# Output projection of a hybrid decoder layer: seven products of sums of quarters in place of eight products of quarters

## The chip, the cores and the metric

The kernel runs on one core of one Trainium2 chip. The metric is device time in microseconds (us). Five engines work side by side, each through its own list of instructions in order: TensorE (PE, matrix products), VectorE (DVE), ScalarE (ACT), GpSimd (POOL, here almost only an issuer of loads) and SyncE (SP, the issuer of most loads). They wait for each other through semaphores.

## What is computed

The layer normalises x (256 tokens, 2048 features), multiplies by one wide input matrix, runs two token mixers beside each other (a gated delta rule and block attention), widens both, merges them through two sigmoid gates and projects the result once more. All of it is float32. The change concerns the last lines:

```python
u_a = oa @ w_branch_a
...
u_b = ob @ w_branch_b
merged = jax.nn.sigmoid(gate_a) * u_a + jax.nn.sigmoid(gate_b) * u_b
return merged @ w_out          # 256 x 2048 times 2048 x 2048
...
x = x + rms_norm(y, post_norm_w[l])
```

## The kernel before

**Split products.** TensorE multiplies in a reduced float32 form (float32r). To keep float32 accuracy each operand is split in a high and a low part: `split` (L218 to L223) lets ScalarE copy the high part (L221) and VectorE subtract it from the whole for the low part (L222). A product of two split operands is three matrix products: high by high, high by low, low by high. The weights pass through three buffers for the high and three for the low parts (pool `wspl`), the raw weights through three buffers of 1 MB (pool `wraw`), loaded by SP.

**The projections with tokens on the partitions** go through `proj_n` (L360 to L377): 512 output columns, two banks of PSUM (one for each tile of 128 tokens). For every four k-tiles (of 128 rows of the weights) one load of 1 MB, in two halves; each half is split once (128 x 1024) and feeds 12 matrix products of 128 x 128 by 128 x 512: two k-tiles, two token tiles, three products each. After every k-tile `tick()` runs the queues of side work, which are Python generators that say after how many k-tiles their next piece comes (a unit is two k-tiles).

**The last stages** are four rounds of two projections, here called ua0, ub0, ... ua3, ub3 (L897 to L905; 8 k-tiles each, 48 products), and the output projection y0 to y3 (L937 to L969; 16 k-tiles, 96 products each). After each ua VectorE multiplies the gate `ga` by its two banks (L900), after each ub it multiplies `gb` by its banks (L903) and adds (L904); that is a quarter of the columns of the merged matrix. `merge(c)` (L884 to L895) then turns this quarter with TensorE (four transposes for each token tile, "mt", L141) and splits it into `mT`, ScalarE the high part (L893) and VectorE the low one (L894). It runs in pieces during the next projection: the second quarter's during ua2, the last one's during y0. So k-tiles 4c to 4c + 3 of the output projection come from `merge(c)`.

The output projection takes its weights through `proj_n` for the column blocks 0 to 2, and `weigh` (L915) squares and weighs the two banks of a block after it (ScalarE L918, VectorE L922, with `postw`, loaded by POOL long before). The last block keeps its split weights and goes through one token tile after the other (L943 to L969), and `finish` adds the residual `hx` (POOL's load) and stores.

**What sets the order.** Products and transposes keep the order in which they are written (`pin`), and so do some operations of the other engines. The rest of VectorE's, ScalarE's and the loads' instructions are put in order by a scheduler when the kernel is built; on the chip each engine follows that order strictly. In its order for the kernel before, both low parts for the first k-tiles of ub2 stand ahead of the multiplications by ua2's banks.

## Time and profile before

| what | value |
| --- | --- |
| runs | 786.99 us median of 3 (786.76 to 787.74) |
| span of the profiled execution, first to last instruction | 786.4 us (its whole time is not recorded; the runs' median lies 0.6 us above this span) |
| busy: TensorE, VectorE, ScalarE | 774.7, 509.6, 403.0 us |
| first product of the output projection starts | 690.19 us |
| loads in all | 143.85 MB read, 187 GB/s over the span |

The profile's page gives busy times, the chain of work that ended last, and groups of instructions; other views of the same trace list instructions in order of time. A row of such a timeline is: start in us, duration in us, engine, line, operation, output<-inputs, shape, and in brackets how long the engine was idle before it and what it had waited for. "PEld" is TensorE's loading of the stationary operand. In a chain the columns are start, duration and work; in a table of windows they are the window, its length, then busy time and count of PE, PEld, DVE, ACT and POOL, the granted clock, the share of DMA and GB/s. Durations overlap a little for instructions in a row on one engine, so the distance from start to start is what one costs.

### The profile page before, as it was taken

How to read it: one execution, taken by the hardware profiler on the slowest of the kernel's cores; microseconds unless marked ns; L12 is line 12 of the kernel's file. 1: busy time of each engine (PE TensorE's matmuls, PEld its weight loads, DVE VectorE, ACT ScalarE, POOL GpSimd, SP SyncE). 2: the span in 40 equal slices, each digit the busy share in tenths (PEclk: the TensorE clock that was granted, in tenths of full speed). 3: DMA queues.
4: the chain of work that ended last, by engine and by line, in shares of the span. 5: the costliest groups of instructions: out<-in, count | busy, mean ns of one | idle time of the engine just before them, and what ended most of it. 6: DMA issues, size and time to landing. Idle time of an engine off the chain costs nothing.

```text
span 786.4 us, 10111 instructions
## 1 busy us (share of the span) xinstructions
PE 774.7 (99%) x3881; PEld 651.8 (83%) x3881; DVE 509.6 (65%) x849; ACT 403.0 (51%) x610; POOL 23.6 (3%) x50
## 2 busy tenths in 40 slices
PE   8999999999999999999999999999999999999995
PEld 6878888888888888888888988888888888888884
DVE  4877886785868898864446565555644666665563
ACT  4777665554745444455355647454454444444451
POOL 3010000100110000020000000000000000000000
PEclk9999999999999999999999999999999999999998
DMA  8756655665596656676435465555455554575542
GB/s 261 252 168 214 186 188 165 198 188 161 174 266 220 210 166 208 199 228 197 117 117 169 153 215 161 182 165 189 161 190 175 175 206 164 196 285 205 172 158 107
DMA packets 94960, 147.67 MB, mean 188 GB/s; under 512 B 5120, under 2 KB 47152, under 8 KB 94272
## 3 DMA queue, kind: packets, MB, share of 16 engines
q1 hardware_dynamic: 92528, 137.50, 54.3%
q0 software_dynamic: 1808, 8.48, 3.9%
q10 hardware_dynamic: 576, 1.05, 0.4%
q8 instruction: 30, 0.49, 0.3%
q14 instruction: 18, 0.15, 0.1%
HBM read 143.85 MB, written 3.17 MB: 187 GB/s over the span
## 4 chain that ended last, share of the span: by engine, by line
PE 96%; DMA 2%; ACT 1%; DVE 0%; SPq 0%; issue 0%; DVEq 0%; ACTq 0%
PE a_ga L138 11%; PE a_gb L138 11%; PE a_y L138 11%; PE a_mk L138 6%; PE a_v L138 6%; PE a_mq L138 6%; PE a_ua L138 6%; PE a_zg L138 6%; PE a_zm L138 6%; PE a_ub L138 6%; PE a_q L138 5%; PE a_k L138 5%; PE a_mv L138 5%; DMA x<-in_x_dram 2%; PE sv L138 2%; PE s L138 1%
## 5 line engine op out<-in xcount | busy, mean ns | idle before, releaser
L138 PE MATMUL a_ga<-hi_ga,hT 128*128 128x512 f32 x256 | 82.2, 394 | 0.0
L138 PE MATMUL a_gb<-hi_gb,hT 128*128 128x512 f32 x256 | 82.1, 394 | 0.0
L222 DVE TENSOR_TENSOR lo_gb<-raw_gb,hi_gb 128x1024 fp32r<-128x1024 f32 x32 | 39.2, 1224 | 41.1 <-ACT hi_gb L221 41.1
L138 PE MATMUL a_y<-hi_y,mT 128*128 128x512 f32 x208 | 65.1, 390 | 0.0
L221 ACT CAST hi_gb<-raw_gb 128x1024 fp32r<-128x1024 f32 x32 | 33.7, 1052 | 48.5 <-PE a_gb L138 34.5
L222 DVE TENSOR_TENSOR lo_ga<-raw_ga,hi_ga 128x1024 fp32r<-128x1024 f32 x32 | 39.0, 1223 | 29.4 <-ACT hi_ga L221 29.4
L221 ACT CAST hi_ga<-raw_ga 128x1024 fp32r<-128x1024 f32 x32 | 33.5, 1051 | 46.3 <-PE a_ga L138 30.3
L138 PEld LDWEIGHTS a_ga<-hi_ga,hT 128*128 128x128 f32 x256 | 48.0, 188 | 11.0 <-issue 1.0
L138 PEld LDWEIGHTS a_gb<-hi_gb,hT 128*128 128x128 f32 x256 | 48.1, 188 | 10.0
L222 DVE TENSOR_TENSOR lo_y<-raw_y,hi_y 128x1024 fp32r<-128x1024 f32 x26 | 31.7, 1224 | 29.6 <-ACT hi_y L221 29.6
L138 PE MATMUL a_ga<-lo_ga,hT 128*128 128x512 f32 x128 | 50.0, 391 | 0.0
L138 PE MATMUL a_gb<-lo_gb,hT 128*128 128x512 f32 x128 | 49.8, 389 | 0.0
L138 PE MATMUL a_k<-hT,hi_k 128*128 128x512 f32 x128 | 46.8, 406 | 0.1
L138 PE MATMUL a_q<-hT,hi_q 128*128 128x512 f32 x128 | 46.6, 404 | 0.0
L138 PE MATMUL a_mk<-hT,hi_mk 128*128 128x512 f32 x128 | 46.1, 401 | 0.0
L138 PEld LDWEIGHTS a_y<-hi_y,mT 128*128 128x128 f32 x208 | 39.0, 188 | 8.1
L138 PE MATMUL a_mq<-hT,hi_mq 128*128 128x512 f32 x128 | 45.7, 400 | 0.0
L138 PE MATMUL a_v<-hT,hi_v 128*128 128x512 f32 x128 | 45.3, 397 | 0.0
L221 ACT CAST hi_y<-raw_y 128x1024 fp32r<-128x1024 f32 x26 | 27.3, 1054 | 34.6 <-PE a_y L138 29.6
L138 PE MATMUL a_ua<-hi_ua,oaT 128*128 128x512 f32 x128 | 41.8, 395 | 0.0
L138 PE MATMUL a_zg<-hi_zg,hT 128*128 128x512 f32 x128 | 40.6, 391 | 0.0
L138 PE MATMUL a_zm<-hi_zm,hT 128*128 128x512 f32 x128 | 40.5, 392 | 0.0
(286 smaller groups left out, 1873.8 us busy)
## 6 DMA issues: line engine op xcount, KB each, us to landing
raw_ga<-in_w_in_dram SPq DMA_DIRECT2D x16, 1024.0 KB, 5.2
raw_gb<-in_w_in_dram SPq DMA_DIRECT2D x16, 1024.0 KB, 5.1
raw_y<-in_w_out_dram SPq DMA_DIRECT2D x16, 1024.0 KB, 5.0
raw_mv<-in_w_in_dram SPq DMA_DIRECT2D x8, 1024.0 KB, 5.5
raw_zg<-in_w_in_dram SPq DMA_DIRECT2D x8, 1024.0 KB, 5.1
raw_v<-in_w_in_dram SPq DMA_DIRECT2D x8, 1024.0 KB, 5.6
raw_zm<-in_w_in_dram SPq DMA_DIRECT2D x8, 1024.0 KB, 5.0
raw_mq<-in_w_in_dram SPq DMA_DIRECT2D x8, 1024.0 KB, 5.7
```

Of the source, the lines that this page charges most:

```text
L138: return pin(nc.tensor.matmul(*args, **kwargs))
L221: nc.scalar.copy(hi, raw)
L222: nc.vector.tensor_tensor(lo, raw, hi.bitcast(F32), op=ALU.subtract)
```

## The change

Of the output projection, the part that belongs to column blocks 0 and 1 and to k-tiles 0 to 7 is a product of 2 x 2 quarters: the token tiles 0 and 1, times the k-tile groups h = 0 and 1, times the column blocks c = 0 and 1. Before, its eight quarter products are part of y0 and y1 (four k-tiles, 12 matrix products each). Now seven products of sums and differences of quarters are made (Winograd's form of Strassen's scheme), and their results are added into the four result banks. The k-tiles 8 to 15 of both blocks, block 2 and block 3 are computed as before.

- `merge(0)` also copies its two token tiles into `sums_f`; `merge(1)` forms four sums of quarters of the merged matrix on VectorE, splits each (ScalarE the high parts, VectorE the low ones), and has POOL load a third quarter of the weights.
- POOL loads two other quarters of the weights earlier, and `differences()`, a queue of its own that is served by the same ticks, makes three differences of quarters on VectorE, in six operations of 128 x 1024.
- `product` does one of the seven products: two halves, each split and fed to 6 matrix products with one token tile; the same function does k-tiles 8 to 15 with both token tiles, 12 matrix products for each split half.
- The results gather in four banks; two are copied out by ScalarE on the way (`s1`, `s5`), VectorE adds into one bank and into `v`, and adds `s1` and `v` back at the end of each block. A fourth difference of weight quarters is made between the products.
- `postw` and `hx` are loaded after these products; POOL's queue holds three loads of 1 MB more, SP's one less.

```diff
     def merge(c):
         yield 1
+        p3s = []
         for t in range(NT):
...
             nc.vector.tensor_tensor(lo, p3, hi.bitcast(F32), op=ALU.subtract)
+            if c == 0:
+                nc.scalar.copy(sf[:, t], p3)
             yield 0.5
+        if c == 1:
+            nc.vector.tensor_tensor(sf[:, 2], p3s[1], sf[:, 1], op=ALU.add)
+            nc.vector.tensor_tensor(sf[:, 3], sf[:, 2], sf[:, 0], op=ALU.subtract)
+            nc.vector.tensor_tensor(sf[:, 1], sf[:, 0], sf[:, 1], op=ALU.subtract)
+            nc.vector.tensor_tensor(sf[:, 0], p3s[0], sf[:, 3], op=ALU.subtract)
+            yield 0.5
+            for i, j in enumerate((2, 3, 1, 0)):
+                nc.scalar.copy(SH[i], sf[:, j])
+                nc.vector.tensor_tensor(SL[i], sf[:, j], SH[i].bitcast(F32), op=ALU.subtract)
+                yield 0.5
+            load_quarter(0, 0, 1)
+            formed.append(True)
+            sq.add(differences())
...
+    load_quarter(1, 1, 1)
+    load_quarter(2, 0, 0)
+
+    def differences():
+        yield 4
+        for o, a, b in ((0, 0, 2), (1, 1, 0), (2, 1, 2)):
+            for u in range(2):
+                us = slice(2 * u, 2 * u + 2)
+                nc.vector.tensor_tensor(tq[o][:, us], tq[a][:, us], tq[b][:, us], op=ALU.subtract)
+                yield 2
...
+    def product(a, raw, banks, first, name):
+        for u in range(2):
+            hi, lo = split(raw[:, 2 * u : 2 * u + 2, :], [P, 2, 512], f"{name}_{u}")
+            for kk in range(2):
+                k = 2 * u + kk
+                for (ah, al), pt, new in zip(a, banks, first):
+                    mm(pt, ah[:, k], hi[:, kk, :], start=(new and k == 0), stop=False, skip_group_check=True)
+                    mm(pt, ah[:, k], lo[:, kk, :], start=False, stop=False, skip_group_check=True)
+                    mm(pt, al[:, k], hi[:, kk, :], start=False, stop=(k == 3), skip_group_check=True)
+                tick()
...
+    product([quarter(0, 0)], load(0, 0), [c21], [True], "yp1")
+    product([s_[0]], tq[0], [c12], [True], "yp5")
+    nc.scalar.copy(s1, c21)
+    raw21 = load(1, 0)
+    product([s_[1]], tq[1], [c21], [False], "yp6")
+    nc.scalar.copy(s5, c12)
+    product([quarter(0, 1)], raw21, [c11], [True], "yp2")
+    nc.vector.tensor_tensor(c12, c21, s5, op=ALU.add)
+    for u in range(2):
+        us = slice(2 * u, 2 * u + 2)
+        nc.vector.tensor_tensor(tq[1][:, us], raw21[:, us], tq[1][:, us], op=ALU.subtract)
+    product([s_[2]], tq[2], [c21], [False], "yp7")
+    product([s_[3]], load(1, 1), [c12], [False], "yp3")
+    nc.vector.tensor_tensor(v, c21, s5, op=ALU.add)
+    product([quarter(1, 1)], tq[1], [c21], [False], "yp4")
...
-    for c in range(3):
-        pts = proj_n(wo, c * 512, mT, KT, f"y{c}")
-        if c < 2:
-            for t in range(NT):
-                weigh(c, t, pts[t])
+    mq.drain()
+    for c, banks, late in ((0, (c11, c21), (c11, s1)), (1, (c12, c22), (c22, v))):
+        for h in range(2, 4):
+            product([quarter(0, h), quarter(1, h)], load(h, c), banks, [False, c == 1 and h == 2], f"y{c}_{h}")
+        nc.vector.tensor_tensor(late[0], late[0], late[1], op=ALU.add)
+        for t in range(NT):
+            weigh(c, t, banks[t])
+    pts = proj_n(wo, 2 * 512, mT, KT, "y2")
```

The products are named after the code: product 1 (yp1), 5, 6, 2, 7, 3, 4, in this order. Each call of `product` names its left factor, its weights and its bank.

More of the change, by code (lines that the diff above doesn't have):

```diff
@@ L128, in hybrid_layer @@
     after = [0]
+    extra = []
     def tick():
         after[0] -= 0.5
-        for q in (gq, vq, mq, *aq):
+        for q in (gq, vq, mq, *aq, *extra):
             q.tick()
@@ L882, in hybrid_layer, with load_quarter @@
     mT = big.tile([P, KT, 2 * S], F32R, tag="hT", name="mT")
+    sums = [big.tile([P, 2, 4, P], F32R, tag=tg, name=f"sum_{tg}") for tg in ("tt", "tv", "tw")]
+    SH = [tl[:, 0] for tl in sums] + [wk.tile([P, 4, P], F32R, tag="s", name="sum4_hi")]
+    SL = [tl[:, 1] for tl in sums] + [wk.tile([P, 4, P], F32R, tag="s", name="sum4_lo")]
+    sf = big.tile([P, 4, 4, P], F32, tag="z0", name="sums_f")
+    tq = [None, None, None]
+    def load_quarter(i, h, c):
+        tq[i] = big.tile([P, 4, 512], F32, tag=f"z{i}", name=f"tq_{i}")
+        nc.gpsimd.dma_start(
+            tq[i], wo[h * 512 : (h + 1) * 512, c * 512 : (c + 1) * 512].rearrange("(k p) c -> p k c", p=P)
+        )
+    load_quarter(1, 1, 1)
[7 more added lines that the diff above has]
+                yield 2
     def merge(c):
         yield 1
+        p3s = []
         for t in range(NT):
@@ L890, in merge @@
             p3 = pt.rearrange("p (k n) -> p k n", n=P)
+            p3s.append(p3)
             hi = mT[:, 4 * c : 4 * c + 4, t * P : (t + 1) * P]
@@ L894, in merge @@
             nc.vector.tensor_tensor(lo, p3, hi.bitcast(F32), op=ALU.subtract)
+            if c == 0:
+                nc.scalar.copy(sf[:, t], p3)
             yield 0.5
+        if c == 1:
[11 more added lines that the diff above has]
+            sq.add(differences())
+    formed = []
+    sq = Queue()
+    extra.append(sq)
     for c in range(D // 512):
@@ L905, in hybrid_layer, with quarter, load @@
         mq.add(merge(c))
+    sq.drain()
+    while not formed:
+        mq.tick()
+    def quarter(t, h):
+        ks = slice(4 * h, 4 * h + 4)
+        return mT[:, ks, t * P : (t + 1) * P], mT[:, ks, S + t * P : S + (t + 1) * P]
+    def load(h, c):
+        raw = wraw.tile([P, 4, 512], F32, tag="raw", name=f"raw_y{c}_{h}")
+        nc.sync.dma_start(raw, wo[h * 512 : (h + 1) * 512, c * 512 : (c + 1) * 512].rearrange("(k p) c -> p k c", p=P))
+        return raw
+    def product(a, raw, banks, first, name):
[8 more added lines that the diff above has]
+                tick()
+    c21, c11, c12, c22 = (acc_tile(f"a_y{n}") for n in ("21", "11", "12", "22"))
+    kept = big.tile([P, 3, 512], F32, tag="u1", name="kept")
+    s1, s5, v = (kept[:, i] for i in range(3))
+    s_ = list(zip(SH, SL))
+    product([quarter(0, 0)], load(0, 0), [c21], [True], "yp1")
[13 more added lines that the diff above has]
+    product([quarter(1, 1)], tq[1], [c21], [False], "yp4")
     postw = big.tile([P, D], F32, tag="z2", name="postw")
```

## The prediction

> **What bounds the kernel now.** I read the page first (busy shares, chain), then the chain in order of time from 600 us on, the windows of the last stages, and the timelines of VectorE (DVE), ScalarE (ACT) and TensorE (PE) around the edit.

> ```profile
> span 786.4 us, 10111 instructions
> ...
> PE 774.7 (99%) x3881; PEld 651.8 (83%) x3881; DVE 509.6 (65%) x849; ACT 403.0 (51%) x610; POOL 23.6 (3%) x50
> ...
> PE 96%; DMA 2%; ACT 1%; DVE 0%; SPq 0%; issue 0%; DVEq 0%; ACTq 0%
> ```

> ```profile
> 656.77 10.88 PE a_ub L138 x48
> ...
> 690.35 2.72 PE a_y L138 x12
> 693.07 0.44 PE mt L141 x4
> ...
> 695.34 83.00 PE a_y L138 x366
> ```

> ```profile
> 644.95:656.77 11.82, 11.82 (x57) 9.79 (x57) 8.48 (x11) 5.29 (x6) 0.00 (x0) 1.00 0.50 177
> 656.77:667.65 10.88, 10.88 (x49) 9.01 (x49) 6.09 (x7) 4.22 (x4) 0.00 (x0) 1.00 0.57 194
> 690.35:712.99 22.64, 22.64 (x105) 18.74 (x105) 13.01 (x14) 10.09 (x12) 0.72 (x1) 1.00 0.77 279
> ```

> TensorE is 96% of the chain, and from 600 us to the last product nothing else stands in it: 366 products take 83.00 us, **0.2268 us each**, also where many in a row go into one bank (the last block). So a product less is 0.227 us less, as long as TensorE never has to wait. The windows say how much room there is: VectorE is busy 8.48 of 11.82 us in the third product with the first branch (ua2), 6.09 of 10.88 in ub2, 13.01 of 22.64 in the first output block.

> **What is removed.** Eight quarter products of 12 matrix products (4 k-tiles, three each) become seven: 12 x 0.2268 = **-2.72 us**. The rest of the chain keeps its products. Everything else in the change is work for VectorE, ScalarE and the queues, and the question is whether TensorE waits for it. It does, at two places.

> **Place one: the start of ub2.** The sums of the quarters of the merged matrix hang on the second merge, which runs during ua2. In the kernel before, this stretch looks like this (VectorE, then TensorE, then ScalarE):

> ```profile
> 649.94 1.35 DVE L894 TENSOR_TENSOR mT<-mt,mT 128x512 fp32r<-128x512 f32 x2
> 652.45 1.23 DVE L222 TENSOR_TENSOR lo_ub<-raw_ub,hi_ub 128x1024 fp32r<-128x1024 f32 x1 [1.17 <-ACT hi_ub L221]
> 655.17 1.23 DVE L222 TENSOR_TENSOR lo_ub<-raw_ub,hi_ub 128x1024 fp32r<-128x1024 f32 x1 [1.50 <-ACT hi_ub L221]
> 656.32 0.68 DVE L900 TENSOR_TENSOR ga<-ga,a_ua 128x512 f32<-128x512 f32 x1
> ```

> ```profile
> 656.38 0.39 PE L138 MATMUL a_ua<-hi_ua,oaT 128*128 128x512 f32 x1
> 656.61 0.39 PE L138 MATMUL a_ub<-hi_ub,obT 128*128 128x512 f32 x1
> ...
> 656.83 0.39 PE L138 MATMUL a_ub<-lo_ub,obT 128*128 128x512 f32 x1
> ```

> ```profile
> 649.98 0.59 ACT L893 CAST mT<-mt 128x512 fp32r<-128x512 f32 x1 [0.73 <-PE mt L141]
> 651.37 1.05 ACT L221 CAST hi_ub<-raw_ub 128x1024 fp32r<-128x1024 f32 x1 [0.80 <-PE a_ua L138]
> 654.09 1.05 ACT L221 CAST hi_ub<-raw_ub 128x1024 fp32r<-128x1024 f32 x1 [1.67 <-PE a_ua L138]
> ```

> Two low parts for ub2 are ready before ua2 ends, and only then come the multiplications by ua2's result (L900), which must wait for ua2's last product. In the order that the scheduler makes of the changed kernel, eight new operations of 512 columns (four sums, four low parts of the sums) stand behind the two mT operations, then **both multiplications, and only behind these the first low part for ub2**. A low part behind an operation that waits for the end of ua2 cannot be early. For its time I need the pitch of VectorE's operations in a row:

> ```profile
> 689.90 1.28 DVE L903 TENSOR_TENSOR gb<-gb,a_ub 128x512 f32<-128x512 f32 x2
> 691.09 1.29 DVE L904 TENSOR_TENSOR ga<-ga,gb 128x512 f32<-128x512 f32 x2
> 692.30 1.22 DVE L222 TENSOR_TENSOR lo_y<-raw_y,hi_y 128x1024 fp32r<-128x1024 f32 x1
> ```

> ```profile
> 760.47 2.35 DVE L955 TENSOR_TENSOR keep_u<-raw_y,keep_u 128x1024 fp32r<-128x1024 f32 x2
> 762.73 2.35 DVE L222 TENSOR_TENSOR lo_y<-raw_y,hi_y 128x1024 fp32r<-128x1024 f32 x2
> ```

> Two operations of 512 take 1.20 us, two of 1024 take 2.26: 0.60 and **1.13 us** from start to start, 0.68 and 1.22 to the end of one. The hand-over from TensorE to ScalarE and the price of a late operand come from these:

> ```profile
> 689.96 0.39 PE L138 MATMUL a_ub<-hi_ub,obT 128*128 128x512 f32 x1
> ...
> 690.19 0.39 PE L138 MATMUL a_y<-hi_y,mT 128*128 128x512 f32 x1
> ...
> 690.39 1.06 ACT L221 CAST hi_y<-raw_y 128x1024 fp32r<-128x1024 f32 x1 [1.67 <-PE a_ub L138]
> ```

> ```profile
> 6.61 0.69 DVE L277 TENSOR_TENSOR lo_k<-rawf_k,hi_k 128x512 fp32r<-128x512 f32 x1
> ...
> 7.35 0.29 PEld L138 LDWEIGHTS a_k<-hT,lo_k 128*128 128x128 f32 x1 [0.44 <-DVE lo_k L277]
> 7.36 0.58 PE L138 MATMUL a_k<-hT,lo_k 128*128 128x256 f32 x1
> ...
> 7.73 0.63 PE L138 MATMUL a_k<-hT,hi_k 128*128 128x512 f32 x1
> ```

> ```profile
> 8.16 0.41 PE L138 MATMUL a_k<-hT,lo_k 128*128 128x256 f32 x1
> 8.37 0.63 PE L138 MATMUL a_k<-hT,hi_k 128*128 128x512 f32 x1
> ```

> A product issued at 689.96 ends at 690.35 and ScalarE starts at 690.39: 0.04 us. A low part that ended at 7.30 let TensorE go on at 7.35: 0.05 us, and the late product held TensorE 0.37 us where the same shape holds it 0.21: up to 0.16 us more, since its weights were not loaded ahead. I take 0.10 for that at the later, faster pace.

> Now the sum for ub2, on the clock of before. The second mT operation waits for its copy (650.57) and starts at 650.61; the sums follow. The last of the four low parts waits for the fourth high copy, which ScalarE does behind hi_ub (654.09 plus a pitch of 0.95): 655.04 to 655.63. So that low part starts at 655.67, the multiplications at 656.27 and 656.87 (ua2's last product ends at 656.77, so without any sums the second would start at 656.81: the order alone carries the wait), the low part for ub2 at 657.47. It ends at 658.69; plus 0.05 and 0.10, the second product of ub2 goes at 658.84 in place of 656.83: **+2.0 us**. VectorE then makes a low part per 1.13 us and TensorE takes one per 12 products, 2.72 us, so the lead is regained.

> **Place two: the seven products.** A half quarter of weights now feeds 6 products (1.36 us) instead of 12 (2.72 us), but still costs VectorE a low part of 1.13 us, and two differences, one sum and two mT operations stand between them. In the changed order, all in one row from 692.30 on (pitches as above; mT 0.65, from the pair's 1.35): lo of product 5 at 692.30, mT 693.43, lo 694.08, mT 695.21, product 6 at 695.86 and 696.99, difference 698.12, product 2 at 699.25 and 700.38, sum 701.51, difference 702.11, first lo of product 7 at **703.24**, end 704.46. ScalarE keeps up: the tightest, the high part for product 6 behind the copy of product 1's bank, is ready at 695.82. With nothing in its way TensorE would want product 7's low part at 702.19 (690.19, four quarter products of 2.72, 0.88 us of mt, one product), so it waits 2.4 us, in pieces, until 704.46 + 0.15 = 704.61. From there 35 products are left (5 of this half, 6, 12, 12): 7.94 us, end of the stage at 712.55. Before, it ended at 690.19 + 22.64 = 712.83. So of the 2.72 us **only 0.3 is left**. The low part for the last product comes just when it is wanted (710.04 against 710.06, behind the sum that reads the bank of product 7); I add 0.1 for that: **-0.2 us**.

> **What costs nothing.** The six differences of quarters during ub2 and ua3 (1.13 each, 6.8 us) and the two late bank sums (0.60) lie in VectorE's gaps: it idles 1.5 us per low part there, as the rows above show in brackets. The first difference waits for a quarter that POOL can only load once the sums are done (656.35):

> ```profile
> hx<-in_x_dram POOLq DMA_DIRECT2D x1, 2048.0 KB, 9.8
> ...
> postw<-in_post_norm_w_dram POOLq DMA_DIRECT2D x1, 1024.0 KB, 4.9
> ```

> At 4.9 us (the load of the same size) it lands at 661.3; that difference and three operations more stand ahead of ua3's first low part, so it is done at 661.3 + 4 x 1.13 + 1.22 = 667.0 and wanted at 656.61 + 2.0 + 10.88 + 0.23 = 669.7. Some 2.5 us of delay are covered. The load of postw moves behind hx on POOL and behind product 7, to about 706, and is wanted some 17 us later. SP issues one load less; POOL's three make 2 MB more in all, with DMA at 0.50 to 0.77.

> **Sum.** +2.0 - 0.2 = +1.8 on the span of 786.4, which is 788.2; runs lie 0.6 above that span (median 786.99): **788.8 us**. Bounds of what before does not show: the late operand 0 to 0.16 at three places that count (-0.3 to +0.2); differences with a plain float32 result between the 1.13 of a low part and twice the 0.60 of a 512-column operation (0 to +0.15 for two); the pitch where 1.15 stands (655.17 to 656.32) over 8 operations, +0.15; ScalarE or the last product later by 0.3; the other way, sums and hand-overs shorter by 0.3; and the runs' own spread, 786.76 to 787.74. That makes 787.9 to 790.2.

> **The rivals.** *The order does not bind at ub2*: were the low part for ub2 made before 655.6, its place in before, place one is free and only -0.2 remains: 786.8, not slower. Against it: the multiplication ahead of it needs a product that ends at 656.77. *It does what it says*: no wait at either place, -2.72, **784.3**. For it only VectorE's 65%; against it the row of 1.13 us against 1.36 us with five more operations between. *The quarter lands late*: at 9.8 us, as hx did, ua3's first low part is 2.4 us late: 791.2. For it, the DMA runs at up to 0.77; against it, 9.8 was for twice the bytes. *TensorE slows after waiting*:

> ```profile
> 27.84 0.28 PE L138 MATMUL a_k<-hT,lo_k 128*128 128x256 f32 x1
> 27.95 0.39 PE L138 MATMUL a_k<-hT,hi_k 128*128 128x512 f32 x1
> ```

> At 8.16 a product of 256 columns held TensorE 0.21 us, at 27.84 only 0.11: there is a slow pace, in the first stage with its gaps. If 2 us of waiting brought it back for as long as from 6.6 to about 14 us, half of that time is lost, 3.8 us: 792.6; if for half as long, 790.7. Against it: the gap is one and short. [...]

> **How the numbers follow.** Forecast 0.67 (787.9 to 790.2); order not binding 0.10; full gain 0.05; late quarter 0.10; slow pace 0.08. A measurement here tells about 0.2%, 1.57 us: from 785.4 to 788.56 is "the same". Of the forecast some two thirds lie above that, 0.46, and with the last two rivals 0.64 is slower; 0.21 + 0.10 is the same; 0.05 faster. The range from 787.9 to 791.4 holds the forecast, the late quarter and half of the slow pace, 0.81.

> **What would show it.** In the changed profile: 84 products where 96 were; TensorE idle about 2.0 us at the second product of ub2, released by VectorE's low part, with both multiplications directly before it; four waits in the seven products, the last and largest (about 1.3 us) before product 7's first low part, and VectorE without a gap for 12 us before it; product pace 0.227 throughout; the loaded quarter landing in about 5 us. I am wrong if ub2 starts without a wait, if VectorE has gaps between the products, or if waits appear in ua3.

## The result, and the profile after

The kernel after takes **789.58 us** (median of 5 runs, 789.03 to 791.4), the kernel before 786.99 us (5 runs beside them, 786.67 to 787.74): a ratio of 1.0034, with a 95% interval of 1.0022 to 1.0046. The change makes it about 2.6 us slower. The profiled execution of after took 789.26 us and its span is 787.5; the runs of every kernel here lie 1.7 to 1.9 us above their own span.

The page of after has 12 products less and 22 us more work on VectorE, and DVE now stands in the chain that ended last, at 2% where it had 0%:

```profile
PE 771.8 (98%) x3869; PEld 647.6 (82%) x3869; DVE 531.5 (67%) x875; ACT 413.3 (52%) x624; POOL 26.2 (3%) x53
...
PE 94%; DVE 2%; SPq 1%; ACT 1%; DMA 1%; issue 1%; DVEq 0%; ACTq 0%
```

Executions begin ua0 up to 1.3 us apart with the same products up to there (1.1 us later in before than in after, so the two spans differ by only 1.1 us). The two traces are therefore laid beside each other from ua0 on. The windows are: ua0's first product to the first product of the output projection; from there to the first product of k-tiles 8 to 15; from there to the end. First before, then after:

```profile
600.19:690.19 90.00, 90.00 (x412) 74.52 (x410) 55.69 (x61) 37.94 (x41) 0.00 (x0) 1.00 0.54 187
690.19:712.83 22.64, 22.64 (x105) 18.78 (x104) 13.16 (x14) 9.93 (x11) 0.72 (x1) 1.00 0.77 279
712.83:778.33 65.50, 65.50 (x289) 53.89 (x288) 34.14 (x36) 27.97 (x38) 0.00 (x0) 1.00 0.46 161
```

```profile
599.08:691.22 92.14, 90.31 (x412) 74.40 (x410) 66.78 (x75) 41.06 (x47) 0.75 (x1) 1.00 0.58 194
691.22:713.94 22.72, 21.13 (x94) 16.17 (x92) 21.97 (x24) 16.67 (x18) 1.27 (x2) 1.00 0.74 273
713.94:779.38 65.44, 65.44 (x289) 53.88 (x287) 36.12 (x39) 28.23 (x38) 0.00 (x0) 1.00 0.48 163
```

Up to the output projection 2.14 us are lost; the seven products take as long as the eight did (22.72 against 22.64), with TensorE idle for 1.6 of them and VectorE busy for 21.97; what follows is unchanged. Sum: 180.30 - 178.14 = +2.2 us.

**The start of ub2**, TensorE and then VectorE of after:

```profile
655.49 0.39 PE L140 MATMUL a_ub<-hi_ub,obT 128*128 128x512 f32 x1
657.71 0.50 PE L140 MATMUL a_ub<-lo_ub,obT 128*128 128x512 f32 x1 [1.83 <-DVE lo_ub L224]
658.04 0.62 PE L140 MATMUL a_ub<-hi_ub,obT 128*128 128x512 f32 x2
```

```profile
654.63 0.69 DVE L942 TENSOR_TENSOR sum_lo<-sums_f,sum_hi 128x512 fp32r<-128x512 f32 x1
655.24 1.28 DVE L955 TENSOR_TENSOR ga<-ga,a_ua 128x512 f32<-128x512 f32 x2
656.43 3.49 DVE L224 TENSOR_TENSOR lo_ub<-raw_ub,hi_ub 128x1024 fp32r<-128x1024 f32 x3
```

The last of the sums' low parts, the two multiplications, and only then the low part for ub2's second product, which is issued 2.22 us after the first in place of 0.23 and holds TensorE 0.33 us (658.04 - 657.71) in place of 0.23.

**The seven products**, VectorE, ScalarE and the TensorE rows that waited:

```profile
693.33 1.22 DVE L224 TENSOR_TENSOR lo_yp<-tq,hi_yp 128x1024 fp32r<-128x1024 f32 x1
694.46 0.68 DVE L930 TENSOR_TENSOR mT<-mt,mT 128x512 fp32r<-128x512 f32 x1
695.07 1.21 DVE L224 TENSOR_TENSOR lo_yp<-tq,hi_yp 128x1024 fp32r<-128x1024 f32 x1
696.20 0.68 DVE L930 TENSOR_TENSOR mT<-mt,mT 128x512 fp32r<-128x512 f32 x1
697.02 2.36 DVE L224 TENSOR_TENSOR lo_yp<-tq,hi_yp 128x1024 fp32r<-128x1024 f32 x2
699.30 1.22 DVE L1003 TENSOR_TENSOR tq<-raw_y,tq 128x1024 f32<-128x1024 f32 x1
700.43 2.35 DVE L224 TENSOR_TENSOR lo_yp<-raw_y,hi_yp 128x1024 fp32r<-128x1024 f32 x2
702.70 0.69 DVE L1000 TENSOR_TENSOR a_y<-a_y,kept 128x512 f32<-128x512 f32 x1
703.30 1.21 DVE L1003 TENSOR_TENSOR tq<-raw_y,tq 128x1024 f32<-128x1024 f32 x1
704.44 2.35 DVE L224 TENSOR_TENSOR lo_yp<-tq,hi_yp 128x1024 fp32r<-128x1024 f32 x2
```

```profile
694.75 0.59 ACT L929 CAST mT<-mt 128x512 fp32r<-128x512 f32 x1 [0.44 <-PE mt L143]
695.45 0.59 ACT L995 COPY kept<-a_y 128x512 f32<-128x512 f32 x1
695.94 2.00 ACT L223 CAST hi_yp<-tq 128x1024 fp32r<-128x1024 f32 x2
```

```profile
692.95 0.63 PE L143 MATMUL mt<-ident,ga 128*128 128x128 f32 x4 [0.21 <-DVE ga L959]
...
701.71 0.50 PE L140 MATMUL a_y<-lo_yp,mT 128*128 128x512 f32 x1 [0.39 <-DVE lo_yp L224]
...
704.33 0.39 PE L140 MATMUL a_y<-hi_yp,sum_tw 128*128 128x512 f32 x1
705.71 0.50 PE L140 MATMUL a_y<-lo_yp,sum_tw 128*128 128x512 f32 x1 [0.99 <-DVE lo_yp L224]
```

VectorE's rows follow each other, but for 0.2 us ahead of 697.02 where it waits for ScalarE's high part (the starts differ by 1.13, 0.61, 1.13, 0.82, 2.28, 1.13, 2.27, 0.60, 1.14), and TensorE waits at the end of this row for product 7's first low part. The idle time in brackets understates a wait: it counts from the end of the row before, 0.39 us after its issue, while the next product is otherwise issued after 0.227 us. From issue to issue the three waits shown cost 0.37, 0.55 and 1.15 us (the last: 705.71 - 704.33 - 0.23). A fourth, 0.07 us before product 6's first low part, does not show as idle time at all. Four products with a new operand hold TensorE for 0.33 to 0.34 us in place of 0.227, another 0.4 us. Together these take 2.6 us, and with that nearly all of the 2.72 us of the removed products. The quarter that POOL loads behind the sums makes nothing wait on TensorE here; it lands in 5.4 us:

```profile
tq<-in_w_out_dram POOLq DMA_DIRECT2D x1, 1024.0 KB, 5.4
```

### The profile page after: what moved, and what is told of

It is laid out like the page before. It is cut to its first block, busy times and chain, and to the rows that moved or that the text cites. A ratio compares the mean times of both kernels' runs of the same rounds, so it can differ in the third digit from the quotient of the medians.

```text
span 787.5 us, 10153 instructions
## 1 busy us (share of the span) xinstructions
PE 771.8 (98%) x3869; PEld 647.6 (82%) x3869; DVE 531.5 (67%) x875; ACT 413.3 (52%) x624; POOL 26.2 (3%) x53
## 3 DMA queue, kind: packets, MB, share of 16 engines
q10 hardware_dynamic: 576, 1.05, 0.4%
## 4 chain that ended last, share of the span: by engine, by line
PE 94%; DVE 2%; SPq 1%; ACT 1%; DMA 1%; issue 1%; DVEq 0%; ACTq 0%
PE a_ga L140 11%; PE a_gb L140 11%; PE a_y L140 10%; PE a_mk L140 6%; PE a_v L140 6%; PE a_mq L140 6%; PE a_zg L140 6%; PE a_zm L140 6%; PE a_ua L140 5%; PE a_q L140 5%; PE a_k L140 5%; PE a_ub L140 5%; PE a_mv L140 5%; PE sv L140 2%; PE s L140 1%; DMA x<-in_x_dram 1%
## 5 line engine op out<-in xcount | busy, mean ns | idle before, releaser
L140 PE MATMUL a_y<-hi_y,mT 128*128 128x512 f32 x144 | 44.8, 389 | 0.0
L140 PE MATMUL a_mv<-hi_mv,hT 128*128 128x512 f32 x128 | 40.5, 392 | 0.0
L140 PE MATMUL a_ub<-hi_ub,obT 128*128 128x512 f32 x128 | 40.1, 389 | 0.0
L140 PE MATMUL a_k<-hT,lo_k 128*128 128x256 f32 x128 | 36.2, 283 | 0.0
## 6 DMA issues: line engine op xcount, KB each, us to landing
raw_ga<-in_w_in_dram SPq DMA_DIRECT2D x16, 1024.0 KB, 5.3
raw_gb<-in_w_in_dram SPq DMA_DIRECT2D x16, 1024.0 KB, 5.1
raw_y<-in_w_out_dram SPq DMA_DIRECT2D x15, 1024.0 KB, 5.1
raw_mv<-in_w_in_dram SPq DMA_DIRECT2D x8, 1024.0 KB, 5.6
raw_zg<-in_w_in_dram SPq DMA_DIRECT2D x8, 1024.0 KB, 5.2
raw_v<-in_w_in_dram SPq DMA_DIRECT2D x8, 1024.0 KB, 5.5
raw_zm<-in_w_in_dram SPq DMA_DIRECT2D x8, 1024.0 KB, 5.1
raw_mq<-in_w_in_dram SPq DMA_DIRECT2D x8, 1024.0 KB, 5.7
```

What stands on the lines that cost most here:

```text
L140: return pin(nc.tensor.matmul(*args, **kwargs))
```

## The experiments

The theory of the prediction: both losses are a matter of VectorE's order and row, at ub2 the order alone (low part behind the multiplications), in the products the row of 1.13 us per operation. The rivals: the sums themselves fill VectorE at ub2; something other than VectorE limits the seven products; TensorE slows after waiting.

**1. Low parts ahead.** Both halves of ub2's first load are split ahead of the multiplications, which are pinned behind them; the sums stay ahead of both.

```diff
         pa = proj_n(wa, c * 512, oaT[0], H, f"ua{c}")
+        ready = split_first(wb, c * 512, f"ub{c}") if c == 2 else None
...
-        pb = proj_n(wb, c * 512, ob_tile(), H, f"ub{c}")
+        pb = proj_n(wb, c * 512, ob_tile(), H, f"ub{c}", ready)
```

> The changed kernel, but the two low parts of ub2's first half load stand ahead of the multiplications by ua2's banks, as they did before; the sums still stand ahead of both. Theory (the wait at ub2 comes from the place of the multiplications and, behind them, from the sums): the wait of 2.0 us in the profile after shrinks to about 0.8, since eight sum operations at 0.6 us still end only about 655 us on the clock of before; time about 1.2 us below the changed kernel, 1.0 to 1.5 above before. If the order alone carries the wait, as the prediction put it: wait 0, 2.0 below the changed kernel. If the wait has another cause (the load of the quarter, the sums' ScalarE copies): wait unchanged, same time as the changed kernel.

788.16 us (787.86 to 789.39, 11 runs), ratio to before 1.0007 (0.9998 to 1.0016). ua0 to the products takes 90.96 us (92.14 after, 90.00 before), the products 22.72. TensorE in this kernel:

```profile
656.29 0.50 PE L140 MATMUL a_ub<-lo_ub,obT 128*128 128x512 f32 x1 [0.63 <-DVE lo_ub L374]
```

```profile
655.02 2.35 DVE L374 TENSOR_TENSOR lo_ub<-raw_ub,hi_ub 128x1024 fp32r<-128x1024 f32 x2
```

1.2 of the 2.1 us go with the order, 0.96 stay. The row from 655.02 holds two low parts; the first ends at 656.24: the two mT operations and the eight operations of the sums stand in front of it (648.61 to 655.02).

**2. The order without the sums.** The kernel before, with both multiplications pinned ahead of ub2's first low part.

```diff
+            pin(nc.vector.tensor_tensor(ga[:, c, t, :], ga[:, c, t, :], pa[t], op=ALU.mult))
...
+        low = nc.vector.tensor_tensor(lo, raw, hi.bitcast(F32), op=ALU.subtract)
+        if name == "ub2_0_0":
+            pin(low)
```

> The kernel before, with nothing changed but the order at ub2: both multiplications by ua2's banks ahead of the first low part for ub2. No sums, no new products. Theory (an in-order VectorE with a low part behind an operation that waits for the end of ua2): TensorE waits 1.9 to 2.0 us at the second product of ub2, time 1.9 above before (ratio about 1.0024). Rival (the sums' work holds VectorE, order is harmless): no wait, ratio 1.000.

789.34 us (788.95 to 789.76, 11 runs) against 787.54: ratio 1.0020 (1.0011 to 1.0030). ua0 to the products takes 92.00 us. VectorE, then TensorE:

```profile
655.70 1.37 DVE L902 TENSOR_TENSOR ga<-ga,a_ua 128x512 f32<-128x512 f32 x2 [4.84 <-PE a_ua L138]
656.99 3.49 DVE L222 TENSOR_TENSOR lo_ub<-raw_ub,hi_ub 128x1024 fp32r<-128x1024 f32 x3
```

```profile
658.26 0.50 PE L138 MATMUL a_ub<-lo_ub,obT 128*128 128x512 f32 x1 [1.69 <-DVE lo_ub L222]
```

VectorE has been idle for 4.84 us and TensorE waits nearly as long as in after. The order alone makes 2.0 us; with 1, the two causes do not add up but lie over each other: the order alone is enough for nearly all of the wait, the sums alone for half of it.

**3. The fourth difference early**, ahead of the seven products, into a tile of its own.

```diff
+    raw11 = load(0, 0)
+    raw21 = load(1, 0)
+    for u in range(2):
+        us = slice(2 * u, 2 * u + 2)
+        nc.vector.tensor_tensor(d4[:, us], raw21[:, us], tq[1][:, us], op=ALU.subtract)
...
-    for u in range(2):
-        us = slice(2 * u, 2 * u + 2)
-        nc.vector.tensor_tensor(tq[1][:, us], raw21[:, us], tq[1][:, us], op=ALU.subtract)
```

> The changed kernel, but the fourth difference of weight quarters is written to a tile of its own, so that it no longer waits for product 6 and can be made in VectorE's gaps during ub3. Theory (VectorE is the bound in the seven products: two operations of 1.13 us fewer in its row ahead of product 7): the waits before products 2 and 7 fall from 0.6 and 1.3 us to 0.0 to 0.3, time 1.7 to 2.1 us below the changed kernel, within 0.6 us of before. Rival (the products wait for ScalarE's high parts or for the loads): time as the changed kernel.

```profile
691.62:712.50 20.88, 20.67 (x93) 16.18 (x92) 19.85 (x22) 16.71 (x18) 1.27 (x2) 1.00 0.82 302
```

The products take 20.88 us instead of 22.72, and the only idle time left to TensorE among them is 0.21 us, for `ga`. Two operations of 1.13 us out of the row give 1.84 us: VectorE's row is what held the seven products. The time moved less: 789.21 us, ratio 1.0016 (1.0007 to 1.0025). Its 11 runs lie in two groups, 787.39 to 788.28 (four runs) and 789.03 to 789.63 us (seven), and the profiled one (787.99) belongs to the lower; experiment 6 says what may part them.

**4. The sums later**, by two steps of the queue, so that ub2's low parts come first.

```diff
         if c == 1:
+            yield 2
             nc.vector.tensor_tensor(sf[:, 2], p3s[1], sf[:, 1], op=ALU.add)
```

> The changed kernel with one line more: the forming of the four sums waits two units of ticks longer, so that the scheduler puts the sums behind ub2's first low parts. Everything is still computed. Theory: no wait at ub2, 2.0 to 2.1 us less than the changed kernel, which leaves place two alone: 787.0 to 787.3, ratio to before 1.000 to 1.001. Rival (the loss sits in the seven products, or the later sums make ua3 wait for the quarter's load): 788.5 to 789.6.

789.02 us (788.42 to 789.96, 11 runs), ratio 1.0018 (1.0009 to 1.0027). The wait at ub2 is gone, and ua0 to the products takes 91.13 us, 1.1 more than in before: half of the loss is back one projection later. VectorE, then TensorE, in ua3:

```profile
666.04 1.23 DVE L915 TENSOR_TENSOR tq<-tq,tq 128x1024 f32<-128x1024 f32 x1 [2.44 <-DMA tq<-in_w_out_dram]
```

```profile
670.34 0.63 PE L143 MATMUL mt<-ident,ga 128*128 128x128 f32 x4 [0.94 <-DVE ga L960]
```

POOL's load stands behind the sums, so it starts later (659.16 against 655.62) and lands in 6.8 us; the first difference waits for it, and the multiplications and the sum that the third merge needs stand behind that difference.

**5. Both, 3 and 4 together.**

> The changed kernel with the sums later and the fourth difference early: both waits taken away, every product and sum kept. Theory: what is left of the waits is 0.3 us of the last merge's transposes in product 1, 0.2 at product 6 and 0.3 at product 7; of the 2.72 us of removed products about 1.8 to 2.0 remain: 785.0 to 785.3, ratio 0.9975. Rival (a third cost that neither wait explains, such as 2 MB more of loads or a slower pace of products): 786.5 or more.

787.32 us (786.86 to 789.94, 12 runs), ratio 0.9997 (0.9989 to 1.0006): no change against before, where a gain of about 2 us was expected. The products take 20.98 us, ua0 to the products 91.58, because VectorE now waits 2.91 us for the quarter and the third merge 1.41 us for VectorE.

**6. More in the row.** Half of the fourth difference is made three times in its place, two operations of 1.13 us more (the second brings back what the first replaced, so the third makes the same difference again, up to rounding).

```diff
-        nc.vector.tensor_tensor(tq[1][:, us], raw21[:, us], tq[1][:, us], op=ALU.subtract)
+        for _ in range(3 if u == 0 else 1):
+            nc.vector.tensor_tensor(tq[1][:, us], raw21[:, us], tq[1][:, us], op=ALU.subtract)
```

> The changed kernel with one half of the fourth difference made three times in place (subtracted, restored, subtracted; the result is the same up to rounding): two VectorE operations of 1024 columns more ahead of product 7, 1.13 to 1.26 us each. Theory (VectorE's row is the bound there): the wait before product 7 grows from 1.3 to 3.7 us, time 2.3 to 2.5 above the changed kernel, 791.7 to 792.1. Rival (VectorE has room there): no change.

793.36 us (793.06 to 795.14, 5 runs), ratio 1.0068 (1.0055 to 1.0081). In the profiled execution (795.14) the products take 26.48 us, 3.76 more than in after, where 2 x 1.13 was added, and ua0 to the products 93.73 instead of 92.14 with the same wait of 1.83 us at ub2. The windows behind the two waits say why (the column after the five engines is the granted clock):

```profile
656.30:659.71 3.41, 1.58 (x7) 1.24 (x7) 3.41 (x5) 1.01 (x1) 0.60 (x1) 1.00 0.53 173
659.71:663.12 3.41, 3.41 (x9) 2.64 (x8) 1.97 (x2) 0.96 (x1) 0.00 (x0) 0.50 1.01 374
663.12:666.53 3.41, 3.41 (x16) 2.82 (x15) 3.29 (x3) 1.14 (x2) 0.00 (x0) 1.00 0.40 112
707.50:710.92 3.42, 0.81 (x4) 0.68 (x5) 3.42 (x4) 0.21 (x1) 0.00 (x0) 1.00 0.19 36
710.92:714.33 3.41, 3.41 (x10) 2.65 (x9) 2.63 (x3) 1.04 (x1) 0.57 (x1) 0.50 1.07 425
```

Twice TensorE runs at **half speed for 3.41 us** (a granted clock of 0.50) and takes 9 or 10 products where 16 go at full speed. The two stretches begin 51.2 us apart, 15 times 3.413, and the half speed that follows the last product sets in 78.5 us after the second began, 23 times 3.413: in this execution the stretches lie on a grid with a step of 51.2 / 15 = 3.413 us. So the rival that TensorE slows after waiting is true here. It seems to be so in the kernel after as well: of its first five runs, those of 789.0 to 789.6 us have a mean clock of 0.997 or 0.998, those of 791 us one of 0.995.

**7. The kernel after, unaltered, again.**

> The changed kernel unaltered, beside its variants on one chip. Theory: 789.2 to 789.6, with waits of 2.0 us at ub2 and 2.3 us in all in the products, in another execution too. Rival (part of the loss comes and goes between executions, such as the landing of the quarter): waits or the landing time of the quarters differ by over 0.3 us.

790.92 us (789.5 to 791.69, 5 runs), ratio 1.0033 (1.0020 to 1.0047): the times spread as in the first five runs, and the 789.2 to 789.6 us that were expected held for one run alone. Two runs have a clock of 0.995 (791.08 and 791.69), but the median itself has 0.997, so the clock is not all that parts the runs. The profiled one (789.5) has the same waits as after (1.83 us at ub2) and the clock at 1.00 from 599 us to the last product.

**8 and 9. Longer waits without sums.** Experiment 2's kernel, with half of the low part computed once (8) or three times (9, with range(3)) more ahead of it, 0.72 us each.

```diff
+        if name == "ub2_0_0":
+            for _ in range(1):
+                pin(nc.vector.tensor_tensor(lo[:, 0], raw[:, 0], hi[:, 0].bitcast(F32), op=ALU.subtract))
```

> The kernel before, with the multiplications by ua2 ahead of the first low part of ub2 (as in the second experiment), and half of that low part (128x512) computed once more ahead of it: TensorE is idle there for 1.69 + 0.72 = 2.4 us instead of 1.69 us; no sums, no seven products. Theory 1 (the length of the idle stretch brings the lower clock: never at 1.69 us, in about half of the executions at 1.83 us): nearly every run has a mean clock of 0.994 to 0.996 and 1.7 us on top of the wait's 0.7: 791.5 to 792.0 us. Theory 2 (it needs the changed kernel's denser work on VectorE and the DMA queues): the wait alone, 790.0 to 790.2 us, and mean clocks of 0.996 to 0.998.

> As the kernel with the 2.4 us wait, but the half is computed three times: TensorE is idle for 1.69 + 3 x 0.72 = 3.85 us. Theory 1 (the length of the idle stretch brings the lower clock): every run at a clock of 0.994 to 0.996, 789.3 + 2.2 + 1.7 = 793.2 us, and a granted clock of 0.7 to 0.8 in the 7 us behind the wait. Theory 2 (the changed kernel's other work brings it): 791.5 us and no such stretch.

8: 789.52 us (788.96 to 790.44, 5 runs), ratio 1.0034 (1.0022 to 1.0047), every clock 0.997 or 0.998. 9: 793.21 us (792.5 to 793.45, 4 runs), ratio 1.0079 (1.0066 to 1.0093), every clock 0.993 to 0.995. The waits are 2.42 and 3.87 us. Windows of 8, then of 9, around the wait:

```profile
654.06:657.47 3.41, 1.60 (x8) 0.98 (x6) 2.64 (x4) 1.04 (x1) 0.00 (x0) 1.00 0.00 0
```

```profile
657.22:660.63 3.41, 0.13 (x1) 0.13 (x2) 3.31 (x5) 0.26 (x1) 0.00 (x0) 1.00 0.00 0
660.63:664.04 3.41, 3.41 (x9) 2.64 (x10) 2.08 (x2) 0.00 (x0) 0.00 (x0) 0.51 0.28 79
```

Neither theory holds as it was put. A wait of 3.87 us in the kernel before brought the half speed too (a clock of 0.51 in the window behind it), so the changed kernel's other work is not needed; but with a wait of 2.42 us none of five runs has a mean clock below 0.997. In the profiled one the grid's edge (placed by the half-speed stretch after the last product, counted back in steps of 3.413) cuts the wait: 1.60 us of the stretch before it were busy. In 9, where both are seen, the half speed behind the wait and that after the last product set in 126.3 us apart, 37 such steps. In 8 the stretch behind the one shown has the clock at 1.00 too. In these two and the next two executions it goes with how much of the wait falls into one stretch: behind 0.13 and 1.58 us of products the clock was 0.51 and 0.50, behind 1.60 and 1.62 it was 1.00.

**10 and 11. The kernel after, two executions side by side.**

> The kernel after, unaltered, one profiled execution: its runs fall into 789.0 to 789.6 us (mean clock 0.997 to 0.998) and 790.9 to 791.7 us (0.995). Theory 1 (the clock is granted for stretches of 3.41 us on a grid that runs by itself, and a stretch that holds nearly all of TensorE's 1.99 us without a product at ub2 is followed by one at half speed): an execution of 789 us has the clock at 1.0 throughout and the edge of a stretch inside the wait; one of 791 us has exactly one half-speed stretch, of 3.4 us, beginning within 2 us of the wait's end, and costs 1.7 us more. Theory 2 (the longer executions lose their 1.7 us at start-up or in the products stage): no half-speed stretch behind ub2's wait.

> The kernel after once more, as in the run before it: Theory 1, at 789 us no stretch at half speed and at 791 us exactly one, of 3.4 us, behind the wait at ub2. Theory 2, no such stretch at either time.

791.26 and 789.88 us: one of each kind, in the same code, with ub2's first two products issued at 655.97 and 658.18 us in the one and 655.96 and 658.17 in the other. Windows on each one's grid, first the longer:

```profile
655.41:658.82 3.41, 1.58 (x8) 1.00 (x7) 3.41 (x5) 1.04 (x1) 0.75 (x1) 1.00 0.30 67
658.82:662.23 3.41, 3.41 (x10) 2.63 (x9) 2.12 (x3) 0.00 (x0) 0.00 (x0) 0.50 1.00 366
```

```profile
654.72:658.14 3.42, 1.62 (x8) 1.01 (x6) 3.29 (x6) 1.38 (x2) 0.75 (x1) 1.00 0.14 18
658.14:661.55 3.41, 3.38 (x15) 2.81 (x16) 2.25 (x2) 0.51 (x1) 0.00 (x0) 1.00 0.93 335
```

In the longer one the whole wait lies in one stretch (TensorE busy 1.58 of 3.41 us), and the next runs at half speed. In the other the edge falls 0.03 us before the wait's end, 1.62 us count as busy, and the clock stays at 1.00. From the late product to the first of the output projection the one takes 35.07 us (658.18 to 693.25), the other 33.69 (658.17 to 691.86): the stretch costs **1.4 us** (1.7 was expected), which is the difference of the two times, 1.38.

**12. All costs moved away.** The sums six steps later, the fourth difference early, shorter steps between the other differences, and the plain sums in the tile that the second and third differences need (the expectation names the third alone), so that the first needs no late load.

```diff
-    sf = big.tile([P, 4, 4, P], F32, tag="z0", name="sums_f")
+    sf = big.tile([P, 4, 4, P], F32, tag="z1", name="sums_f")
...
-    load_quarter(1, 1, 1)
+    load_quarter(0, 0, 1)
...
-        yield 4
+        yield 1
...
-                yield 2
+                yield 1
...
         if c == 1:
+            yield 6
...
-            load_quarter(0, 0, 1)
+            load_quarter(1, 1, 1)
...
+    raw11 = load(0, 0)
+    raw21 = load(1, 0)
+    for u in range(2):
+        us = slice(2 * u, 2 * u + 2)
+        nc.vector.tensor_tensor(d4[:, us], raw21[:, us], tq[1][:, us], op=ALU.subtract)
```

> The kernel after with three edits: the sums of the second merge are formed six steps later, between the first parts of ub2 instead of ahead of them; the fourth difference is made ahead of the products, into a tile of its own; and the tile of the plain sums is that of quarter (1,1), so that only the third difference waits for the late load and quarters (0,1) and (0,0) lie ready for the first. Theory (each of the three costs found so far is a matter of order and placing on VectorE, and the removed products then come out whole): ua0 to the products 90.0 us as before, the products stage 20.9 to 21.0 us instead of 22.64, and no wait of more than 0.4 us in ua3; 1.7 to 2.0 us less than before, 785.5 to 785.9 us. Rival (the seven products cost VectorE more than there is room for, wherever the work is put): a wait of 1 to 2 us appears at a new place, 787.0 to 788.0 us.

785.83 us (785.11 to 786.18, 11 runs) against 786.86 (786.14 to 788.22, 15 runs): ratio **0.9985** (0.9976 to 0.9994), a little faster than the kernel before, where after is slower. Its three windows, cut as those of before and after:

```profile
598.94:688.93 89.99, 89.99 (x411) 74.56 (x410) 68.89 (x77) 41.04 (x47) 0.75 (x1) 1.00 0.59 204
688.93:709.86 20.93, 20.67 (x94) 16.17 (x92) 19.87 (x22) 16.70 (x18) 1.27 (x2) 1.00 0.84 299
709.86:775.30 65.44, 65.44 (x289) 53.91 (x287) 36.16 (x39) 28.21 (x38) 0.00 (x0) 1.00 0.48 162
```

ua0 to the products takes as long as in before, with 13 us more of VectorE's work in it; the products take 1.71 us less. So the same arithmetic, in another order, gives 1.8 us in the profile instead of costing 2.2. The medians show 1.0 of it; their interval reaches from 0.5 to 1.9 us. The other 1.0 us of the 2.72 is still lost in the products: 0.4 of it, from issue to issue, to the merge that waits for `ga` (0.26 us idle), and another 0.4 to products with a new operand, three of which hold TensorE for 0.33 to 0.34 us.

## Why the prediction was right or wrong, point by point

The forecast of 788.8 us came out 0.8 us low, and slower as it said; the measured 789.58 us lie inside its range. (The bounds that it lists add up to 788.0 to 790.3 us where it writes 787.9 to 790.2.) Its step of 0.6 us from span to time joins the span of one execution with the median of others: a run here lies 1.7 to 1.9 us above its own span, so the profiled execution of before, whose span is 786.4, was a long one. That does no harm, because the +1.8 us are in effect added to the median.

- **What is removed** held: 3869 products in place of 3881, and the unchanged rest takes 65.44 us against 65.50, so the pace is the same.
- **Place one** held: +2.0 was forecast, +2.14 measured, with the rows in the order that it named and the late product holding TensorE 0.10 us longer, as taken. "The order alone carries the wait" is shown by experiment 2 (+2.0 without any sum). What the prediction did not say is that the sums alone would leave 0.96 (experiment 1).
- **Place two** has the failed terms: -0.2 was forecast, +0.08 measured. The start of VectorE's row came exactly as said, 2.11 us after the stage began. Then "ScalarE keeps up: the tightest, the high part for product 6 ..., is ready at 695.82" missed by a little: it was to be ready 5.63 us into the stage and was so after 5.77 (695.94 + 1.05), since ScalarE did the second mT copy, the copy of product 1's bank and this high part in one row, and the first of them waited for the transposes. VectorE waited, and product 7's first low part began 13.22 us into the stage instead of 13.05. The other 0.1 was lost behind that product and was not followed further. The mechanism, the row of 1.13 us, is shown by experiment 3 (two operations out, -1.84) and 6. Of its signs, the four waits came, the last and largest before product 7 (about 1.3 us was named; 1.15 from issue to issue, 1.26 with the longer hold). VectorE's row had one gap, of 0.2 us, where none was to be.
- **The quarter's load** was covered, as said: 5.4 us against 4.9, and TensorE did not wait. That its slack is limited shows in experiment 4: there the quarter is issued 3.5 us later and lands 4.9 us later, and waits appear in ua3. The 2.5 us themselves were not measured.
- **The rival of the slow pace** was put at 0.08 and is part of the result: by their clock (0.995) two of the five runs have it, though not the median one (0.997). Its price was taken as 1.9 to 3.8 us, from the first stage; it is 1.4, since it lasts one stretch of 3.41 us (experiments 10 and 11). Against it the prediction held that the gap is one and short; in experiment 10 one gap of 1.83 us was enough, in a stretch in which TensorE was busy for 1.58 of 3.41 us. Behind the short waits among after's products, of up to 0.99 us, the clock was 1.00 in all four profiled executions of that kernel.
- **The sum**: +2.2 in the profile where +1.8 was forecast, of which 0.3 is place two and 0.1 place one. The median lies 2.6 above before's; the 0.4 us between are within what runs of one kernel differ by, and no profile explains them.

**Open:** why none of five runs shows the half speed in its clock (0.997 or 0.998) with the wait of 2.42 us (experiment 8), when its place on the grid should have allowed it in many; part of an answer may be that the places are not evenly spread. Counted back from where the half speed sets in after the last product, the edges of seven of the fourteen profiled executions lie within 0.3 us of each other, measured from the span's start, experiment 8's among them, and an edge there cuts that wait; but seven of fourteen does not explain five of five. Nor is the limit known. In the stretches around the waits, 1.58 us of products brought the half speed and 1.60 did not (the edges are good to some 0.07 us), but after the last product of experiment 4 a stretch with only 1.49 us was not followed by one at half speed either; that came one stretch later:

```profile
777.01:780.42 3.41, 1.49 (x7) 0.91 (x5) 1.07 (x4) 0.98 (x3) 0.00 (x0) 1.00 0.00 0
780.42:783.84 3.42, 0.00 (x0) 0.00 (x0) 2.63 (x5) 0.00 (x0) 0.00 (x0) 1.00 0.58 219
```

So the busy time of TensorE, as these profiles give it, does not alone decide. That the upper group of experiment 3's runs (clock 0.994 in five of the seven) is the same stretch is argued from the clock and the same wait at ub2, not shown: none of them was profiled. A low mean clock is no proof: one run of the kernel before, which has no such wait, has 0.995 too (789.21 us, beside experiments 5 to 7), and one of experiment 5 has 0.994 (789.94 us), whose longest wait in the profile is 1.41 us.

## What to carry to other kernels

Where a change takes products from TensorE and gives operations to another engine, write that engine's order down, operation by operation with its pitch, around the places where TensorE starts on new weights: the busy share over the whole span (65%) said there was room, the row at two places said there was none. The same work can then often be put where the row has gaps; here it turned a loss of 2.2 us in the profile into a gain of 1.8. After each move ask what stood behind the moved work on every engine: moving the sums moved a load, and the load's wait came out as large as the one removed.
